# Attention of a fused encoder trunk: samples taken two by two, a head pair's values beside the scores of pair p+2, and scores and values of the same tile shape in one visit of TensorE

## The chip, the cores and the metric

The kernel runs on one core of one Trainium2 chip. The metric is device time in microseconds (us) of one execution. Engines are called as the profile calls them: PE (TensorE), DVE (VectorE), ACT (ScalarE), POOL (GpSimd) and SP (SyncE, which issues DMAs).

## The reference

Two layers of an encoder trunk, on 512 tokens of one prompt and 8 x 16 tokens of eight running samples (640 tokens of width 1024) with shared weights. Cut to what matters:

```python
# per layer: x += SwiGLU_1(norm(x))/2 ; mixer ; x += SwiGLU_2(norm(x))/2
z = h @ w_in          # conv B | C | V, q | k | v, two gates
def _band_attention(q, k, v, q_pos, k_pos, rel_bias):
    s = jnp.einsum('bqhd,bkhd->bhqk', q, k) * (HEAD_DIM ** -0.5)
    s = s + rel_bias[:, idx][None]
    s = jnp.where(valid[None, None], s, NEG_INF)     # chunk-causal band
    p = jax.nn.softmax(s, axis=-1)
    return jnp.einsum('bhqk,bkhd->bqhd', p, v)
# prompt: 512 queries on their own 512 keys; 8 heads of 64
# sample b: 16 queries on 256 cached keys and its 16 new ones
m = sigmoid(g_c) * (y_c @ w_conv_out) + sigmoid(g_a) * (y_a @ w_attn_out)
x += m @ w_o
```

## The kernel before

All is fp32. A large product is made of three: each operand is split into a high part (hi) and a rest (lo), and PE adds hi*hi, lo*hi and hi*lo (`block`, L395). Weights come in slabs: SP loads a `raw` block (L245, three buffers), ACT casts it to `whi` (L305), DVE subtracts to get `wlo` (L310, in one or two pieces), and some slabs are sums of blocks (L249, tiles `raw` and `s`). PE takes a whole layer's products as such slabs of 128x128 weights over two halves of 320 tokens; `seven` makes a 2x2 block product of seven half-size ones, with DVE adding the partial results (L249, for instance `g <- mb_g`) and ACT copying them (L716, L724, L728).

Attention is woven into this. Inside the mixer PE's order is the order in which the code is written. The other engines' order is made by a scheduler from priorities: `soon()` raises one by 300, a weight slab has 150. `attention()` holds a generator, `stream`, with all products that don't hang on attention (q and k of head pairs 1 to 3, the convolutions, the gates), cut in 140 steps of six matmuls of 128x320. `fill(n)` lets PE run n steps. Between fills PE visits attention. The eight heads go in four pairs, the two heads of a pair in two halves of the array:

- `scores(p)`: q x k for the row blocks 0 to 3 of 128 queries, 128 to 512 keys wide, on tiles of 64 rows by 128 columns (L1669). The results (`pss`) are read by DVE, which adds the bias and takes the maximum (L1675); then the negative maximum (L1826), ACT's exponentials (L1828), DVE's reciprocal (L1831), and ACT's scaling (L1686). Odd pairs hold them in tiles `s`, even pairs in `yc`.
- `values(p)`: transposes of the weights (L1699) in two stops of 14 and 6, copied out to `pt` by DVE (first head) and ACT (second, L1702). Then values x weights, here called PV, on tiles of 128 rows by 64 columns (L1713, result `py`, copied by ACT at L1715).
- `sscores(b)`: a sample's scores, tiles of 128x32 (L1757, `spss`); its caches `kc`, `vc` and new values `vn` are loaded on SP (L1746, L1749, L1752), in the queue that also loads the weights.
- `svalues(b)`: three transposes (L1779, L1781, `sptp`), copied out by ACT and DVE (L1783, L1784); then the values of the 16 new keys on tiles of 16x32 and of the cached keys on tiles of 128x32 (both L1791, `spy`), ACT's scaling, and a transpose (L1797, `ptx`, one bank for four samples).

All attention results share four PSUM banks (`att`), in turn; the stream's `ma`, `mb`, `mc` and the scores of row block 1 have the four others (`pr`). The profile lists each of these fp32 attention matmuls as two records, and joins neighbours of one shape on the timeline ("x16"). Before, the prompt's order per pair is scores(p+1), four steps, transposes, two steps, transposes, two steps, PV, six steps. A sample's is four steps, transposes, three steps, then in one visit the scores of sample b+2 and the values of sample b, two steps, last transpose.

Of the kernel before, what the change touches and what calls it, by code (L numbers as in the profile page):

```python
# [12 lines left out]
AF = mybir.ActivationFunctionType  # L13
# [3 lines left out]
P = 128  # L17
D = 1024
L = 2
SEQ = 512  # L20
NB = 8
TS = 16
T = SEQ + NB * TS
HT = T // 2
PAST = 256
H = 8
HD = 64
# [153 lines left out]
def trunk(ctx: ExitStack, tc: tile.TileContext, xin, wst, small, pbias, samplebias, kcache, vcache,  # L181
          yout, ko, vo, co):
    nc = tc.nc
    PE, DVE, ACT, POOL, SP = nc.tensor, nc.vector, nc.scalar, nc.gpsimd, nc.sync
# [8 lines left out]
    ps = ExitStack()  # L193
# [15 lines left out]
    def att(name):  # L209
        return banks["att"].tile([P, 512], F32, tag="att", name=name)  # L210
# [15 lines left out]
    for kind, inside in kinds():  # L226
        n = len(fourth)
# [137 lines left out]
    def soon():  # L365
        return tc.high_priority(offset=300)
# [34 lines left out]
    ident = cp.tile([P, P], F32, name="ident")  # L401
# [12 lines left out]
    for k in range(KT):  # L414
# [4 lines left out]
        if k % 2 == 0:  # L419
            c = slice(k * P, (k + 2) * P)  # L420
# [693 lines left out]
    def mixer(l, after):  # L1114
        with tc.tile_pool(name=f"yp{l}", bufs=1, reuse_waits="tile") as yp, \
# [19 lines left out]
            with tc.tile_pool(name=f"mp{l}", bufs=2, reuse_waits="tile") as mp:  # L1135
# [63 lines left out]
                with tc.manual_schedule(engines={mybir.EngineType.PE}):  # L1199
                    attention(l, h, st, stats, ops, mp, yas, ycp, both, others())  # L1200
# [368 lines left out]
    def attention(l, h, norms, stats, ops, mp, yas, ycp, both, others):  # L1569
# [3 lines left out]
        npair = H // 2  # L1573
        nt = T // P
        NQ = SEQ // P
        KS = PAST + TS
# [29 lines left out]
        def fill(n):  # L1606
            for _ in range(n):
                next(stream, None)
# [5 lines left out]
        for c in range(KT // 2):  # L1614
            wh, wl = chunk()
            for kk in range(2):
# [29 lines left out]
        def scores(p):  # L1646

            heads = [2 * p + e for e in range(2)]
            bias, ss, st = [], [], []
            for hh in heads:  # L1650
                n = f"{l}_{hh}"
                bias.append(mp.tile([P, SEQ], F32, name=f"bias{n}", tag="bias"))
                POOL.dma_start(bias[-1], pbias[l, hh])
                POOL.memset(bias[-1][0:CHUNK, SEQ - CHUNK :], NEG)

                ss.append(mp.tile([P, offs[-1] + SEQ], F32, name=f"s{n}", tag="s") if p % 2
                          else ycp[hh % 2].rearrange("p a t -> p (a t)"))
                st.append(mp.tile([P, 4, NQ], F32, name=f"st{n}", tag="st", bufs=4))

            for rows in ((0, 2), (3,), (1,)):  # L1660
                pss = [(pr if rows == (1,) else att)(f"pss{l}_{hh}_{rows[0]}") for hh in heads]
                spans, o = [], 0
                for i in rows:
                    spans.append((i, slice(o, o + (i + 1) * P)))
                    o = spans[-1][1].stop
                for i, c in spans:
                    for e in range(2):
                        r = slice(e * HD, (e + 1) * HD)
                        PE.matmul(pss[e][:, c], qa[p][r, i * P : (i + 1) * P], ka[p][r, : (i + 1) * P],  # L1669
                                  start=True, stop=True)  # L1670
                for i, c in spans:
                    for e in range(2):
                        w = (i + 1) * P
                        with soon():
                            DVE.tensor_tensor_reduce(  # L1675
                                out=ss[e][:, offs[i] : offs[i] + w], in0=pss[e][:, c],
                                in1=bias[e][:, SEQ - w :], scale=1.0, scalar=NEG, op0=ALU.add,
                                op1=ALU.max, accum_out=st[e][:, 0, i : i + 1])
            for e, hh in enumerate(heads):
                weigh(hh, ss[e], st[e])  # L1680

        def weigh(hh, s, st):
            parts = [(offs[i], (i + 1) * P) for i in range(NQ)]
            softmax(s, st, parts)
            for i, (o, w) in enumerate(parts):
                ACT.activation(s[:, o : o + w], s[:, o : o + w], AF.Copy, scale=st[:, 3, i : i + 1])  # L1686
            weights[hh] = s

        def values(p):

            pt = [mp.tile([P, offs[-1] + SEQ], F32, name=f"pt{l}_{2 * p + e}", tag="pt") for e in range(2)]
            at = [sum(P * (NQ - i) for i in range(j)) for j in range(NQ)]

            def turn(j, e):
                w = (NQ - j) * P
                s = weights[2 * p + e]
                ptp = att(f"ptp{l}_{2 * p + e}_{j}")[:, :w]
                for i in range(j, NQ):
                    PE.transpose(ptp[:, (i - j) * P : (i - j + 1) * P],  # L1699
                                 s[:, offs[i] + j * P : offs[i] + (j + 1) * P], ident)  # L1700
                with soon():
                    (ACT.copy if e else DVE.tensor_copy)(pt[e][:, at[j] : at[j] + w], ptp)  # L1702

            for j in range(NQ):
                for e in range(2):
                    turn(j, e)
                if j % 2:
                    yield
            py = att(f"py{l}_{p}")
            for j in range(NQ):  # L1710
                for e in range(2):
                    hh = 2 * p + e
                    PE.matmul(py[e * HD : (e + 1) * HD, j * P :], vs[j][:, hh * HD : (hh + 1) * HD],  # L1713
                              pt[e][:, at[j] : at[j] + (NQ - j) * P], start=j == 0, stop=j == NQ - 1)
            ACT.copy(yas[:, p, 0:SEQ], py)  # L1715
# [24 lines left out]
        def sscores(b):  # L1740
# [28 lines left out]
                    ACT.activation(early, st[:, 3, 0:1], AF.Sigmoid)  # L1769
            held[b] = box, st, vraw, vn  # L1770

        def svalues(b):
            n = f"{l}_{b}"
            box, st, vraw, vn = held[b]
            s = box[:, :KS]
            pt = box[:, KS : KS + 2 * P].rearrange("p (a b) -> p a b", a=2)
            pn, yx = (box[:n, KS + o * P : KS + (o + 1) * P] for n, o in ((TS, 2), (P, 3)))
            ptp = att(f"sptp{n}")
            for j in range(2):  # L1779
                PE.transpose(ptp[:, j * P : (j + 1) * P], s[:, j * P : (j + 1) * P], ident)  # L1780
            PE.transpose(ptp[:TS, 2 * P : 3 * P], s[:, PAST:], ident)  # L1781
            with soon():
                ACT.copy(pt, ptp[:, : 2 * P].rearrange("p (a b) -> p a b", a=2))  # L1783
                DVE.tensor_copy(pn, ptp[:TS, 2 * P : 3 * P])  # L1784
            yield

            pys = att(f"spy{n}")[:, :P]
            for j, (w, v) in enumerate(((pn, vn), (pt[:, 0], vraw[:, 0]), (pt[:, 1], vraw[:, 1]))):
                for p in range(npair):
                    r = slice(32 * p, 32 * p + 32)  # L1790
                    PE.matmul(pys[r], w[:, r], v[:, p * P : (p + 1) * P], start=j == 0, stop=j == 2)  # L1791
# [6 lines left out]
            if b % G == G - 1:  # L1798
                c0 = SEQ + (b + 1 - G) * TS
                for e in range(2):  # L1800
                    r = slice(e * HD, (e + 1) * HD)
                    with soon():
                        (ACT.copy if e else DVE.tensor_copy)(
                            yas[r, :, c0 : c0 + G * TS].rearrange("p a (b t) -> p a b t", b=G),
                            ptx[0][r].rearrange("p (b a e t) -> p a b e t", b=G, a=npair, e=2)[:, :, :, e, :])

        sscores(0)
        sscores(1)
        for b in range(NB):
            vals = svalues(b)  # L1810
            fill(4)
            next(vals)
            fill(3)
            if b + 2 < NB:
                sscores(b + 2)
            next(vals)
            fill(2)
            next(vals, None)
        fill(KT * KT)

    def softmax(s, st, parts):
# [304 lines left out]
```

## Time and profile before

| | us |
|---|---|
| median of 3 runs (2495.63 to 2496.84) | 2496.47 |
| the profiled execution, whole | 2496.66 |
| its span, first to last instruction | 2494.7 |
| PE busy | 2478.1 |
| DVE busy | 2119.2 |
| ACT busy | 1450.0 |
| POOL busy | 370.7 |

The profiled execution is 1.96 us longer than its span, and 0.19 us above the median. The granted TensorE clock is 0.998 of full speed. Busy time of PE is modelled from pipelined matmuls, so a busy PE need not run at its peak; the distance from the start of one matmul to the start of the next shows that. The woven part of layer 0 lies at about 475 to 650 us of the span, that of layer 1 some 1233 us later.

### The profile page before, as it was taken

What the parts mean: (1) busy time and instruction counts of PE and PEld (TensorE: products, weight loads), DVE (VectorE), ACT (ScalarE), POOL (GpSimd) and SP (SyncE); (2) the same over time, 40 slices, a digit from 0 to 9 for tenths busy, and PEclk for the clock granted to TensorE, in tenths of its full rate; (3) what the DMA queues carried; (4) which work ended last, traced back from release to release, by engine and by line L of the source; (5) the groups of instructions that cost most, each with busy time, mean ns of one, the idle gap of its engine ahead of it and who ended that gap; (6) DMA issues with size and microseconds to landing.
All of it is one profiled execution on the core that took longest, in us unless ns stands there. A gap on an engine that the chain in (4) does not pass through costs nothing.

```text
span 2494.7 us, 43515 instructions
## 1 busy us (share of the span) xinstructions
PE 2478.1 (99%) x17048; PEld 2419.0 (97%) x17048; DVE 2119.2 (85%) x3322; ACT 1450.0 (58%) x2343; POOL 370.7 (15%) x445
## 2 busy tenths in 40 slices
PE   9999999999999999999999999999999999999998
PEld 8999999888999999999999999998899999999998
DVE  7888888878888899888798889888788888989887
ACT  7455556674666555555565555556646665555554
POOL 0011211211111011111001111221111110111111
PEclk9999999999999999999999999999999999999999
DMA  4245665335345344655435555643344553455554
GB/s 146 82 107 124 138 135 130 106 115 167 99 119 145 101 116 118 138 135 135 117 90 126 129 134 123 138 119 115 125 153 104 126 141 95 119 133 122 129 135 110
DMA packets 133261, 308.10 MB, mean 124 GB/s; under 512 B 12768, under 2 KB 76128, under 8 KB 133056
## 3 DMA queue, kind: packets, MB, share of 16 engines
q1 hardware_dynamic: 68976, 219.18, 27.3%
q0 software_dynamic: 63360, 85.50, 20.6%
q8 instruction: 133, 2.18, 0.4%
q10 hardware_dynamic: 720, 0.65, 0.1%
q14 instruction: 72, 0.59, 0.1%
HBM read 221.13 MB, written 7.94 MB: 92 GB/s over the span
## 4 chain that ended last, share of the span: by engine, by line
PE 94%; DVE 3%; ACT 2%; DMA 1%; issue 0%; SPq 0%; DVEq 0%; ACTq 0%
PE pab L395 12%; PE paa L395 11%; PE pcb L395 6%; PE pca L395 6%; PE daa L962 5%; PE dab L962 5%; PE po L372 4%; PE qa L395 4%; PE pbb L395 3%; PE pba L395 3%; PE dca L962 3%; PE dcb L962 3%; PE pda L372 2%; PE pv L1622 2%; PE ma_cv L395 2%; PE qc L395 2%
## 5 line engine op out<-in xcount | busy, mean ns | idle before, releaser
L310 DVE TENSOR_TENSOR wlo<-raw,whi 128x512 fp32r<-128x512 f32 (+1 forms) x583 | 598.6, 1030 | 236.1 <-ACT whi L305 230.6
L305 ACT CAST whi<-raw 128x512 fp32r<-128x512 f32 (+1 forms) x583 | 519.9, 897 | 348.0 <-PE pbb L395 44.6
L305 ACT CAST whi<-s 128x1024 fp32r<-128x1024 f32 (+1 forms) x164 | 153.6, 937 | 248.1 <-issue 107.8
L395 PE MATMUL pab<-xhib,whi 128*128 128x320 f32 x704 | 218.3, 310 | 0.4 <-DVE gb L249 0.4
L395 PE MATMUL pab<-xhib,wlo 128*128 128x320 f32 x704 | 217.4, 309 | 0.0
L395 PE MATMUL pab<-xlob,whi 128*128 128x320 f32 x704 | 217.4, 309 | 0.0
L395 PE MATMUL paa<-xhia,whi 128*128 128x320 f32 x640 | 198.0, 309 | 0.2 <-DVE ga L249 0.2
L395 PE MATMUL paa<-xloa,whi 128*128 128x320 f32 x640 | 197.6, 309 | 0.0
L395 PE MATMUL paa<-xhia,wlo 128*128 128x320 f32 x640 | 197.6, 309 | 0.0
L310 DVE TENSOR_TENSOR wlo<-s,whi 128x1024 fp32r<-128x1024 f32 (+1 forms) x164 | 176.6, 1077 | 10.4 <-ACT whi L305 10.4
L395 PEld LDWEIGHTS pab<-xhib,whi 128*128 128x128 f32 x704 | 132.2, 188 | 1.1 <-DVE gb L249 0.9
L395 PEld LDWEIGHTS pab<-xlob,whi 128*128 128x128 f32 x704 | 132.2, 188 | 0.2
L395 PEld LDWEIGHTS pab<-xhib,wlo 128*128 128x128 f32 x704 | 132.2, 188 | 0.0
L395 PEld LDWEIGHTS paa<-xhia,whi 128*128 128x128 f32 x640 | 120.2, 188 | 0.5 <-DVE ga L249 0.5
L395 PEld LDWEIGHTS paa<-xloa,whi 128*128 128x128 f32 x640 | 120.2, 188 | 0.1
L395 PEld LDWEIGHTS paa<-xhia,wlo 128*128 128x128 f32 x640 | 120.2, 188 | 0.0
L249 DVE TENSOR_TENSOR raw<-raw,raw 128x512 f32<-128x512 f32 x164 | 112.2, 684 | 1.8 <-DMA raw<-in_wst 0.2
L249 DVE TENSOR_TENSOR raw<-s,raw 128x512 f32<-128x512 f32 x164 | 112.3, 685 | 0.0
L395 PE MATMUL pcb<-xhib,whi 128*128 128x320 f32 x352 | 108.7, 309 | 0.0
L395 PE MATMUL pcb<-xlob,whi 128*128 128x320 f32 x352 | 108.7, 309 | 0.0
L395 PE MATMUL pcb<-xhib,wlo 128*128 128x320 f32 x352 | 108.7, 309 | 0.0
L986 POOL DMA_DIRECT2D x<-c_b x52 | 62.6, 1203 | 309.5 <-ACT c_b L979 134.5
(816 smaller groups left out, 8170.8 us busy)
## 6 DMA issues: line engine op xcount, KB each, us to landing
raw<-in_wst SPq DMA_DIRECT2D x375, 512.0 KB, 3.7
x<-c_b POOLq DMA_DIRECT2D x52, 320.0 KB, 5.1
x<-c_a POOLq DMA_DIRECT2D x50, 320.0 KB, 5.0
kc<-in_kcache SPq DMA_DIRECT2D x32, 256.0 KB, 4.1
vc<-in_vcache SPq DMA_DIRECT2D x16, 512.0 KB, 4.5
ub<-cbb POOLq DMA_DIRECT2D x42, 160.0 KB, 5.9
ua<-cba POOLq DMA_DIRECT2D x38, 160.0 KB, 5.4
x<-u_a POOLq DMA_DIRECT2D x18, 320.0 KB, 5.1
```

The costliest lines, as they stand in the source:

```text
L249: DVE.tensor_tensor(out=out, in0=a, in1=b, op=ALU.add)
L305: ACT.copy(hi[:, d], src[:, c])
L310: DVE.tensor_tensor(out=lo, in0=src, in1=hi.bitcast(F32), op=ALU.subtract)
L372: PE.matmul(ps[a] if isinstance(ps, list) else ps[:, a, :HT], w, x[:, a * HT : (a + 1) * HT], start=first and j == 0, stop=last and j == 2)
L395: PE.matmul(ps, a, b, start=start and kp == 0 and j == 0, stop=stop and kp == NP - 1 and j == 2, skip_group_check=True)
L962: PE.matmul(ps[u], w, y, start=start and i == 0 and j == 0, stop=i == 1 and j == 2, skip_group_check=True)
L986: POOL.dma_start(rows(r, cols), z, accum_op=ALU.add)
L1622: PE.matmul(pv[t], xx[:, t * P : (t + 1) * P], w[:, kk * AW : (kk + 1) * AW], start=c == 0 and kk == 0 and j == 0, stop=c == KT // 2 - 1 a ...
```

## The change

Five edits in `attention()`:

1. `scores` takes the row blocks in the order 0, 2, 1, 3 (before 0, 2, 3, 1).
2. The copy of `py` gets the raised priority.
3. PV of pair p is put off: it stands right ahead of scores(p+2), with no step between; PV of the last pair stands right ahead of the first two samples' scores. The transposes keep their places relative to the scores.
4. Samples go in pairs. One visit holds the scores of samples b+2 and b+3, the values of the cached keys of b and b+1, and then those of their new keys.
5. `ptx` holds two samples instead of four, so it is copied out four times per layer instead of twice (by DVE and ACT each time).

The number of steps, of products and of DMAs is the same. Cut to its core:

```diff
@@ scores(p) @@
-            for rows in ((0, 2), (3,), (1,)):
+            for rows in ((0, 2), (1,), (3,)):
...
@@ the end of values(p) @@
-            ACT.copy(yas[:, p, 0:SEQ], py)
+            with soon():
+                ACT.copy(yas[:, p, 0:SEQ], py)
             yield
@@ the schedule of the prompt @@
+        vals = None
         fill(2)
         scores(0)
         fill(14)
         for p in range(npair):
+            if vals:
+                next(vals)
             if p + 1 < npair:
                 scores(p + 1)
-                fill(4)
+            fill(4 if p + 1 < npair else 2)
             vals = values(p)
             next(vals)
             fill(2)
             next(vals)
-            fill(2)
-            next(vals)
-            fill(6)
+            fill(8)
+        next(vals)
...
-        G = 4
+        G = 2
@@ svalues: of one sample before, of two now @@
-        def svalues(b):
...
-            ptp = att(f"sptp{n}")
-            for j in range(2):
-                PE.transpose(ptp[:, j * P : (j + 1) * P], s[:, j * P : (j + 1) * P], ident)
-            PE.transpose(ptp[:TS, 2 * P : 3 * P], s[:, PAST:], ident)
-            with soon():
-                ACT.copy(pt, ptp[:, : 2 * P].rearrange("p (a b) -> p a b", a=2))
-                DVE.tensor_copy(pn, ptp[:TS, 2 * P : 3 * P])
+        def svalues(bs):
...
+            for b, box, pt, pn in zip(bs, boxes, pts, pns):
+                s = box[:, :KS]
+                ptp = att(f"sptp{l}_{b}")
...
+                with soon():
+                    ACT.copy(pt, ptp[:, : 2 * P].rearrange("p (a b) -> p a b", a=2))
+                    DVE.tensor_copy(pn, ptp[:TS, 2 * P : 3 * P])
             yield
-            pys = att(f"spy{n}")[:, :P]
-            for j, (w, v) in enumerate(((pn, vn), (pt[:, 0], vraw[:, 0]), (pt[:, 1], vraw[:, 1]))):
-                for p in range(npair):
-                    r = slice(32 * p, 32 * p + 32)
-                    PE.matmul(pys[r], w[:, r], v[:, p * P : (p + 1) * P], start=j == 0, stop=j == 2)
-            with soon():
-                ACT.activation(yx, pys, AF.Copy, scale=st[:, 3, 0:1])
+            pys = [att(f"spy{l}_{b}")[:, :P] for b in bs]
+            for js in ((0, 1), (2,)):
+                for b, ps, pt, pn in zip(bs, pys, pts, pns):
+                    vraw, vn = held[b][2:]
+                    for j in js:
+                        w, v = (pn, vn) if j == 2 else (pt[:, j], vraw[:, j])
+                        for p in range(npair):
+                            r = slice(32 * p, 32 * p + 32)
+                            PE.matmul(ps[r], w[:, r], v[:, p * P : (p + 1) * P], start=j == 0, stop=j == 2)
+            for b, ps, yx in zip(bs, pys, yxs):
+                with soon():
+                    ACT.activation(yx, ps, AF.Copy, scale=held[b][1][:, 3, 0:1])
             yield
-            if b % G == 0:
-                ptx[0] = att(f"ptx{n}")
-            PE.transpose(ptx[0][:, (b % G) * P : (b % G + 1) * P], yx, ident)
...
+            for b, yx in zip(bs, yxs):
+                if b % G == 0:
+                    ptx[0] = att(f"ptx{l}_{b}")[:, : G * P]
+                PE.transpose(ptx[0][:, (b % G) * P : (b % G + 1) * P], yx, ident)
...
@@ the schedule of the samples @@
         sscores(0)
         sscores(1)
-        for b in range(NB):
-            vals = svalues(b)
+        fill(7)
+        for b in range(0, NB, 2):
+            vals = svalues((b, b + 1))
+            next(vals)
+            fill(5)
+            for c in range(b + 2, min(b + 4, NB)):
+                sscores(c)
+            next(vals)
             fill(4)
-            next(vals)
-            fill(3)
-            if b + 2 < NB:
-                sscores(b + 2)
-            next(vals)
-            fill(2)
             next(vals, None)
+            fill(9 if b + 2 < NB else 0)
         fill(KT * KT)
```

The lines of the changed kernel lie 1 lower from the copy of `py` on, 3 from the samples' loads on, up to 7 and 9 in `svalues`, and 10 from the softmax on: L1760 is `spss`, L1798 is `spy`, L1836 is the negative maximum.

First, PE in layer 0 where the scores of sample 2 are taken (`ma0_b0`, `mc0_b0` are the stream's products, `spss0_2` the scores of sample 2, `spy0_0` the values of sample 0, `vc` its cached and `vn` its new ones). Before:

```order
3282 L395 MATMUL ma0_b0_6175<-thi0_1_4685,wlo147_6142 128x320
3283 L1757 MATMUL spss0_2_6229<-kc0_2_0_6219,bd0_4707 32x272 x2
3284 L1757 MATMUL spss0_2_6229<-kc0_2_1_6221,bd0_4707 32x272 x2
3285 L1791 MATMUL spy0_0_6240<-vn0_0_6095,ss0_0_6104 32x128 x4
3286 L1791 MATMUL spy0_0_6240<-vc0_0_6093,ss0_0_6104 32x128 x8
3287 L395 MATMUL ma0_b0_6175<-thi0_2_4687,whi147_6141 128x320
```

After:

```order
3326 L395 MATMUL mc0_b0_6220<-hhim0_7_4652,wlo148_6172 128x320
3327 L1760 MATMUL spss0_2_6288<-kc0_2_0_6278,bd0_4707 32x272 x2
3328 L1760 MATMUL spss0_2_6288<-kc0_2_1_6280,bd0_4707 32x272 x2
3329 L1760 MATMUL spss0_3_6309<-kc0_3_0_6299,bd0_4707 32x272 x2
3330 L1760 MATMUL spss0_3_6309<-kc0_3_1_6301,bd0_4707 32x272 x2
3331 L1798 MATMUL spy0_0_6320<-vc0_0_6121,ss0_0_6132 32x128 x8
3332 L1798 MATMUL spy0_1_6321<-vc0_1_6142,ss0_1_6153 32x128 x8
3333 L1798 MATMUL spy0_0_6320<-vn0_0_6123,ss0_0_6132 32x128 x4
3334 L1798 MATMUL spy0_1_6321<-vn0_1_6144,ss0_1_6153 32x128 x4
3335 L395 MATMUL ma0_b0_6175<-thi0_0_4683,whi149_6203 128x320
```

Two samples' scores and values stand in one run without a stream matmul between, and the new keys' matmuls have moved behind the cached keys'.

Second, DVE in layer 0 where it works on the scores of pair 1 (`pss0_2`, `pss0_3` are the scores of its two heads, the number behind a row block; `st` holds maxima and sums; ACT's exponentials wait for the row of L1826, now L1836). Before:

```order
627 L1675 ISA s0_2_5270,st0_2_5271<-pss0_2_1_5293,bias0_2_5267 128x256
628 L1675 ISA st0_2_5271 128x1
629 L1675 ISA s0_3_5275,st0_3_5276<-pss0_3_1_5294,bias0_3_5272 128x256
630 L1675 ISA st0_3_5276 128x1
631 L1826 TENSOR_SCALAR st0_2_5271<-st0_2_5271 128x4
632 L310 TENSOR_TENSOR wlo132_5251<-raw74_5184,whi132_5250 128x1024
633 L1826 TENSOR_SCALAR st0_3_5276<-st0_3_5276 128x4
```

After:

```order
626 L1675 ISA s0_2_5270,st0_2_5271<-pss0_2_3_5293,bias0_2_5267 128x512
627 L1675 ISA st0_2_5271 128x1
628 L310 TENSOR_TENSOR wlo131_5227<-raw75_5220,whi131_5226 128x512
629 L1836 TENSOR_SCALAR st0_2_5271<-st0_2_5271 128x4
630 L1675 ISA s0_3_5275,st0_3_5276<-pss0_3_3_5294,bias0_3_5272 128x512
631 L1675 ISA st0_3_5276 128x1
632 L310 TENSOR_TENSOR wlo132_5251<-raw74_5184,whi132_5250 128x1024
633 L1836 TENSOR_SCALAR st0_3_5276<-st0_3_5276 128x4
```

The last row block is now the widest, the first head's negative maximum stands ahead of the second head's last block, and a piece of the weight slab `wlo131` stands ahead of that.

Third, DVE in layer 0 at the first gate's products (`wlo163` is the second weight slab of that block, `g0_0` the gate, `mb0_g0` its second product on PE). Before:

```order
867 L310 TENSOR_TENSOR wlo163_6932<-s6_90_6927,whi163_6931 128x512
868 L1189 TENSOR_TENSOR b0_2_6779<-b0_2_6779,rrm0_4681 128x640
869 L1149 SCALAR_TENSOR_TENSOR b0_3_6780<-ma0_b2_6786,rrm0_4681 128x320
870 L1190 TENSOR_TENSOR yc0_4682<-yc0_4682,b0_2_6779 128x640
871 L1193 TENSOR_TENSOR yc0_4682<-yc0_4682,b0_3_6780 128x640
872 L1784 COPY ss0_6_6744<-sptp0_6_6949 16x128
873 L310 TENSOR_TENSOR wlo163_6932<-raw91_6925,whi163_6931 128x512
874 L249 TENSOR_TENSOR raw90_6889<-s6_90_6927,raw90_6889 128x512
875 L249 TENSOR_TENSOR g0_0_6958<-mb0_g0_6979,capsm0_4680 128x320
876 L310 TENSOR_TENSOR wlo164_6962<-raw90_6889,whi164_6961 128x1024
```

After:

```order
872 L249 TENSOR_TENSOR raw91_6930<-raw91_6930 128x512
873 L249 TENSOR_TENSOR g0_0_6957<-mb0_g0_6978,capsm0_4680 128x320
874 L310 TENSOR_TENSOR wlo163_6937<-s6_90_6932,whi163_6936 128x512
875 L310 TENSOR_TENSOR wlo163_6937<-raw91_6930,whi163_6936 128x512
876 L249 TENSOR_TENSOR raw90_6890<-s6_90_6932,raw90_6890 128x512
```

The sum `g0_0<-mb0_g0`, which waits for PE to end `mb0_g0`, stood behind both pieces of `wlo163` and now stands ahead of both. Layer 1 has the same two orders at this place.

More of the change, by code (lines that the diff above doesn't have):

```diff
@@ L1770, in sscores @@
             held[b] = box, st, vraw, vn
-        def svalues(b):
[L1773 to L1777, printed above, removed]
-            ptp = att(f"sptp{n}")
-            for j in range(2):
-                PE.transpose(ptp[:, j * P : (j + 1) * P], s[:, j * P : (j + 1) * P], ident)
-            PE.transpose(ptp[:TS, 2 * P : 3 * P], s[:, PAST:], ident)
-            with soon():
-                ACT.copy(pt, ptp[:, : 2 * P].rearrange("p (a b) -> p a b", a=2))
-                DVE.tensor_copy(pn, ptp[:TS, 2 * P : 3 * P])
-            yield
-            pys = att(f"spy{n}")[:, :P]
-            for j, (w, v) in enumerate(((pn, vn), (pt[:, 0], vraw[:, 0]), (pt[:, 1], vraw[:, 1]))):
-                for p in range(npair):
-                    r = slice(32 * p, 32 * p + 32)
-                    PE.matmul(pys[r], w[:, r], v[:, p * P : (p + 1) * P], start=j == 0, stop=j == 2)
-            with soon():
-                ACT.activation(yx, pys, AF.Copy, scale=st[:, 3, 0:1])
-            yield
-            if b % G == 0:
-                ptx[0] = att(f"ptx{n}")
-            PE.transpose(ptx[0][:, (b % G) * P : (b % G + 1) * P], yx, ident)
[L1798 to L1805, printed above, removed]
```

14 lines of the change are left out of this document (added).

## The prediction, made before the changed kernel was run

> **What bounds the kernel now.** I read the page first: the span, the busy shares and the chain that ended last.
>
> ```profile
> span 2494.7 us, 43515 instructions
> PE 2478.1 (99%) x17048; PEld 2419.0 (97%) x17048; DVE 2119.2 (85%) x3322; ACT 1450.0 (58%) x2343; POOL 370.7 (15%) x445
> ...
> PE 94%; DVE 3%; ACT 2%; DMA 1%; issue 0%; SPq 0%; DVEq 0%; ACTq 0%
> ```
>
> PE is all but never idle, and 94% of the chain is PE's. Then I read what PE waits for.
>
> ```profile
> PE poa L372 <- ACT whi L618: 5.6, 1, 5.6
> ...
> PE ptp L1699 <- ACT pt L1702: 0.8, 4, 0.3
> ```
>
> The columns are us in total, times, longest. The largest wait lies outside attention; in attention only the transposes wait, four times. So time is gained or lost where PE's own run of matmuls gets shorter or where a new wait holds it. A busy PE says little, so next I read PE's timeline by starts: how far apart are two starts, and how does that change around a visit to attention? This is the PV visit of pair 0.
>
> ```profile
> 499.44 0.31 PE L395 MATMUL ma_qk<-thi,wlo 128*128 128x320 f32 x1
> ...
> 500.32 0.31 PE L395 MATMUL ma_qk<-thi,wlo 128*128 128x320 f32 x1
> 500.56 2.37 PE L1713 MATMUL py<-pt,v 128*64 128x512 f32 x16
> 502.87 0.42 PE L395 MATMUL mc_qk<-hhim,whi 128*128 128x320 f32 x1
> 503.12 0.31 PE L395 MATMUL mc_qk<-hlom,whi 128*128 128x320 f32 x1
> ```
>
> Six starts from 499.44 to 500.32 make 0.147 us for a stream matmul. Into the visit the distance is 0.24, and behind it the first stream matmul takes 0.25 to the next start: 0.09 and 0.10 us too much. So a visit has a price of its own beside its work. The samples' visits show the price inside.
>
> ```profile
> 561.83 0.31 PE L395 MATMUL mc_cv<-hhim,wlo 128*128 128x320 f32 x1
> 562.07 1.12 PE L1757 MATMUL spss<-kc,bd 128*32 128x272 f32 x16
> 563.12 0.41 PE L395 MATMUL ma_cv<-thi,whi 128*128 128x320 f32 x1
> ```
> ```profile
> 569.58 0.31 PE L395 MATMUL ma_b<-thi,wlo 128*128 128x320 f32 x1
> 569.81 0.67 PE L1757 MATMUL spss<-kc,bd 128*32 128x272 f32 x8
> 570.41 0.42 PE L1791 MATMUL spy<-vn,ss 16*32 16x128 f32 x8
> 570.76 0.64 PE L1791 MATMUL spy<-vc,ss 128*32 128x128 f32 x16
> 571.34 0.42 PE L395 MATMUL ma_b<-thi,whi 128*128 128x320 f32 x1
> 571.59 0.31 PE L395 MATMUL ma_b<-tlo,whi 128*128 128x320 f32 x1
> ```
>
> Sixteen records of `spss` take 1.05 to the next start, eight take 0.60: eight more cost 0.45, and 0.15 is left over for going to the next shape. Eight records of `spy` on 16x32 take 0.35, sixteen on 128x32 take 0.58: 0.23 for eight, 0.12 left over. I take 0.13 for leaving a shape; then eight records of `spss` are 0.46 and eight of `spy` 0.22.
>
> **The change part by part**, for one layer; both layers have the same code.
>
> *Samples, three full visits.* One visit of before is 571.59 - 569.58 less two stream matmuls, 1.72; two are 3.43. The paired visit has one way in (0.08), 16 `spss` (0.92), 32 `spy` of cached keys in the same tile shape (0.90), 16 of new keys (0.45), two leavings (0.26) and one way out (0.10): 2.71. It saves 0.72, three times 2.17. That the pair's 48 records of one shape carry no price between `spss` and `spy` is an assumption; if they paid 0.13, 0.4 would be lost.
>
> *Samples, the last pair, without new scores.* One is 0.08 + 0.22 + 0.13 + 0.45 + 0.13 + 0.10 = 1.11, two 2.22; the pair is 0.08 + 0.90 + 0.13 + 0.45 + 0.13 + 0.10 = 1.79: 0.43.
>
> *Prompt.* Three visits go: PV of pairs 0 and 1 join scores, PV of pair 3 the first samples' scores. A join saves a way in and a way out, 0.09 + 0.10, if going directly from one shape to the next costs the 0.13 of a leaving. No row shows 128x64 followed by 64x128. The ends are 0.32 (free) and 0 (as dear as in, leaving and out). I take 0.19, as the small shapes beside each other are the nearest rows: 0.57. The Trainium skill, TensorEngine Tiling (Array Packing), Key Properties, says that a change of tiling mode drains the TensorE and a change of tile alone does not. By that rule alone, with one price for every change, in and out are two drains of 0.16 and a join saves 0.48 in place of 0.57; the trace agrees that each change costs, but puts the price mostly at the 128x128 side.
>
> Transposes are moved, not shortened, and I count nothing for them. So the switches give 2.17 + 0.43 + 0.57 = 3.17.
>
> *Stalls that may go.* The second stop of transposes and one visit of scores:
>
> ```profile
> 498.04 0.83 PE L1699 MATMUL ptp<-ident,yc 128*128 128x128 f32 x6
> 498.63 0.39 PE L395 MATMUL ma_qk<-thi,whi 128*128 128x320 f32 x1
> ```
> ```profile
> 517.63 0.38 PE L1699 MATMUL ptp<-ident,s 128*128 128x128 f32 x2
> 518.17 0.70 PE L1699 MATMUL ptp<-ident,s 128*128 128x128 f32 x4 [0.17 <-ACT pt L1702]
> 518.63 0.40 PE L395 MATMUL ma_qk<-thi,whi 128*128 128x320 f32 x1
> ```
> ```profile
> 537.76 0.38 PE L1699 MATMUL ptp<-ident,yc 128*128 128x128 f32 x2
> ...
> 538.87 0.39 PE L395 MATMUL ma_cv<-thi,whi 128*128 128x320 f32 x1
> ```
> ```profile
> 528.12 0.31 PE L395 MATMUL ma_cv<-hhim,wlo 128*128 128x320 f32 x1
> 528.49 2.43 PE L1669 MATMUL pss<-k,q 64*128 64x128 f32 x16
> ```
>
> Pair 0 needs 0.59 for its six, pair 1 1.00, pair 2 1.11: stalls of 0.41 and 0.52, waits for ACT's copies. The scores of pair 3 begin 0.37 after the matmul ahead instead of 0.24: 0.13. Why are the copies late?
>
> ```profile
> 508.22 1.81 DVE L310 TENSOR_TENSOR wlo<-raw,whi 128x512 fp32r<-128x512 f32 x2
> 509.95 0.28 DVE L1675 CUSTOM_DVE_ANT_0 yc<-pss,bias 128x128 f32<-128x128 f32 x1
> ```
> ```profile
> 513.43 0.40 ACT L1828 ACTIVATE yc<-yc,st 128x128 f32<-128x128 f32 x1 [4.55 <-DVE st L1826]
> ```
>
> DVE is at `wlo` until 509.95 while PE began these scores about 508.3, and ACT, idle for 4.55, begins its exponentials only at 513.43; the copies queue behind them. With PV ahead of the scores PE gives DVE 2.3 us for that `wlo`, and the first head's maximum no longer stands behind the second head's last block. Against it, ACT now scales four blocks ahead of the copies rather than two. The ends are 0 and 0.41 + 0.52 + 0.13 = 1.06; I take 0.70, as DVE's gain of up to 1.6 is the larger. If the cover is not there the stalls stay.
>
> *A stall that comes.* At the first gate `g <- mb_g` now stands ahead of `wlo163` on DVE. PE and DVE there, before, and the duration of such a piece:
>
> ```profile
> 632.24 0.31 PE L395 MATMUL ma_g<-thi,whi 128*128 128x320 f32 x1
> ...
> 632.53 0.31 PE L395 MATMUL ma_g<-thi,wlo 128*128 128x320 f32 x1
> ```
> ```profile
> 632.51 0.49 DVE L249 TENSOR_TENSOR g<-mb_g,capsm 128x320 f32<-128x320 f32 x1 [1.60 <-PE mb_g L395]
> 632.91 1.22 DVE L310 TENSOR_TENSOR wlo<-raw,whi 128x1024 fp32r<-128x1024 f32 x1
> ```
> ```profile
> L310 DVE TENSOR_TENSOR wlo<-s,whi 128x512 fp32r<-128x512 f32 x44 | 30.3, 689 | 7.2 <-ACT whi L305 7.2
> ```
>
> The sum starts when `mb_g` has ended (632.51), the next on DVE at 632.91, and a piece of `wlo` takes 0.69: ready at 633.60. PE wants it in its third matmul, 632.53. That is 1.1 us of standing still, on the path; behind it on DVE wait the second piece and the next slab. Ends 0.7 (a piece starting early and pipelined) and 1.8 (both pieces).
>
> *The rest costs nothing that I can see.* Two more small copies of `ptx` on DVE and ACT per layer lie beside PE's stream; uncovered, four of the size of the sum above would be 2 us per layer. POOL's copies of the samples' keys and its loads of the bias move with the scores; POOL is busy for 15% of the span, and nothing on PE's list waits for it. SP's loads keep their number; their place is a rival below.
>
> The sum per layer is -3.17 - 0.70 + 1.10 = -2.77, twice -5.5. The profiled execution took 2496.66, so 2491.1; the median lies 0.19 lower: **2490.9 us**.
>
> **The rivals.**
>
> *Copies out of PSUM become the limit.* `att` has four banks. In scores(2) and scores(3) the second head's last block takes the bank of `py`, which PE has just filled, and waits for ACT's copy.
>
> ```profile
> 556.73 0.59 ACT L1715 COPY ya<-py 128x512 f32<-128x512 f32 x1 [1.91 <-PE py L1713]
> ```
>
> For it: the copy takes 0.59, and on ACT a cast of a slab stands ahead of it. Against: about half of the scores' 2.3 us, 1.2 to 1.4, lies between PV and that block, so ACT may be 0.6 late unpunished. If it is 1 us later, four visits lose 4 us; with the stalls kept instead, 1.4 is lost. Both leave a gain of about 2 to 4: 2493.5. The Trainium skill, TensorEngine Tiling (Array Packing), PSUM Bottleneck, speaks against the change in this sense: tiling speeds up TensorE and not the evacuation of PSUM, and the copies may become the limit.
>
> *The switches give more and the stall stays small.* Direct changes are free (0.39 more per layer), the stalls go whole (0.36) and the gate waits for 0.7: 3.17 + 0.39 + 1.06 - 0.7 = 3.92 per layer, 2488.6; without the gate's wait 2487.2.
>
> *Weights come late: slower.* On SP the weights' `raw` loads stand behind the samples' loads, which wait for buffers that a visit frees.
>
> ```profile
> SPq L1746 <- PE spss L1757: 51.3, 8, 7.6
> ```
>
> Two samples' loads now wait for one later visit. If the `raw` behind them are late, PE stands at the next slab. For it: waits of up to 7.6 us on that queue. Against: PE's list shows no wait for a weight there, so 7.6 are covered. To end 5 us slower, six paired visits (three per layer) would have to lose (5.5 + 5) / 6 = 1.75 us each, so the queue would have to hold the `raw` that much longer than its cover; 1.9 each gives 2502.3.
>
> **How the numbers follow.** A measurement of this kernel can tell about 0.2%, 5.0 us, from no change. The forecast gets 0.58, the copies' rival 0.22, the larger gain 0.13, late weights 0.07. The forecast's own range is 2489.4 (all three stalls gone, the gate's wait 0.7) to 2492.3 (none gone); the bound of 2491.5 lies in it, so I give 0.45 of its 0.58 to faster, and 0.13 to same. Faster 0.45 + 0.13 = 0.58; same 0.13 + 0.22 = 0.35; slower 0.07. The range 2487.2 to 2494.6 goes from the larger gain to the copies' rival with one more us lost.
>
> **What would show it right or wrong.** Right: on PE's timeline a paired sample visit of about 2.7 us without stream matmuls, and about 1.8 for the last; PV followed by scores at once with less than 0.35 between the last PV start and the first score beyond its own work; the six transposes of pairs 1 and 2 near 0.6; and `ma_g` waiting for `wlo` L310 in PE's waits, about 1.1, twice. Wrong: a start-to-start price of 0.3 or more at each shape change inside a visit; `pss` waiting for `py`'s copy; `whi` or `raw` in PE's list of waits at the samples; or a granted clock below 0.998.

## The result and the profile after

The changed kernel is slower by a little: 2500.93 us median (2499.94 to 2502.43, 17 runs) against 2496.54 (2495.6 to 2497.3, 17 runs), a ratio of 1.0018 with a 95% interval of 1.0011 to 1.0024. Forecast were 2490.9 and a range of 2487.2 to 2494.6. The profiled execution took 2501.16 us, its span is 2499.4.

The page of the changed kernel, the lines shown of before:

```profile
span 2499.4 us, 43503 instructions
PE 2474.7 (99%) x17048; PEld 2422.0 (97%) x17048; DVE 2119.0 (85%) x3326; ACT 1453.0 (58%) x2347; POOL 366.3 (15%) x445
...
PE 90%; DVE 5%; ACT 3%; issue 1%; DMA 1%; SPq 0%; DVEq 0%; ACTq 0%
```

PE's busy time fell by 3.4 us while the span grew by 4.7. PE has less to do and stands still more; in the chain that ended last, PE's share went from 94 to 90%, and that of DVE and ACT rose by 3 points together. What PE waits for (us in total, times, longest):

```profile
PE poa L372 <- ACT whi L618: 5.6, 1, 5.6
PE ma_qk L395 <- DVE k L249: 4.1, 4, 1.0
PE ma_cv L395 <- DVE yc L249: 2.1, 2, 1.1
...
PE ma_g L395 <- DVE wlo L310: 0.8, 2, 0.4
...
PE ma_g L395 <- ACT whi L305: 0.6, 2, 0.3
```

The wait of the transposes for `pt` has gone from this list; four lines are new. The wait at `ma_g` for `wlo` was forecast, that for `whi` and those at `ma_qk` and `ma_cv` were not. The last two are six waits, three per layer, 1.0 to 1.1 each. The first of them on PE, DVE and ACT:

```profile
498.24 0.93 PE L1699 MATMUL ptp<-ident,yc 128*128 128x128 f32 x6
498.93 0.39 PE L395 MATMUL ma_qk<-thi,whi 128*128 128x320 f32 x1
...
500.77 0.41 PE L395 MATMUL mc_qk<-hhim,whi 128*128 128x320 f32 x1
...
502.49 0.31 PE L395 MATMUL mc_qk<-hhim,wlo 128*128 128x320 f32 x1
503.81 0.42 PE L395 MATMUL ma_qk<-thi,whi 128*128 128x320 f32 x1 [1.01 <-DVE k L249]
504.06 0.31 PE L395 MATMUL ma_qk<-tlo,whi 128*128 128x320 f32 x1
```
```profile
498.66 0.69 DVE L1702 COPY pt<-ptp 128x256 f32<-128x256 f32 x2 [0.86 <-PE ptp L1699]
502.13 1.23 DVE L310 TENSOR_TENSOR wlo<-raw,whi 128x1024 fp32r<-128x1024 f32 x1 [2.78 <-ACT whi L305]
503.27 0.48 DVE L249 TENSOR_TENSOR k<-ma_qk,c 128x320 f32<-128x320 f32 x1
```
```profile
500.61 0.54 ACT L1702 COPY pt<-ptp 128x256 f32<-128x256 f32 x2
501.03 1.06 ACT L305 CAST whi<-raw 128x1024 fp32r<-128x1024 f32 x1
```

Read them from the bottom. ACT, with exponentials, scalings and the copies of the transposes ahead, casts a weight slab only at 501.03. DVE has nothing to do for 2.78 us, because the `wlo` of that slab is next in its order. Behind it stands the sum `k<-ma_qk`, whose operand PE had finished by about 500.9. PE wants to write the next product into the same bank at 502.64, may at 503.81 (1.17 too late), and loses another 0.10 on the step after that. In the kernel before the same sum stood behind the same `wlo`, but PV lay between the transposes and this point (500.56 to 502.87 in the rows of the prediction), and PE came to the bank later than the sum ended:

```profile
499.60 1.04 ACT L305 CAST whi<-raw 128x1024 fp32r<-128x1024 f32 x1
```
```profile
502.54 0.48 DVE L249 TENSOR_TENSOR k<-ma_qk,c 128x320 f32<-128x320 f32 x1
```
```profile
504.73 0.31 PE L395 MATMUL ma_qk<-thi,whi 128*128 128x320 f32 x1
```

All three rows are of before. The sum ended at about 502.95, PE came at 504.73: 1.8 to spare. Afterwards 1.2 are lacking, and two things make the difference: PE comes 2.1 sooner (502.64 instead of 504.73), and the sum, behind a cast that starts 1.4 later (501.03 instead of 499.60), starts 0.7 later (503.27 instead of 502.54, where a sum of raw blocks stood between).

The visits themselves came out as forecast:

```profile
507.29 0.31 PE L395 MATMUL ma_qk<-hhim,wlo 128*128 128x320 f32 x1
507.52 2.38 PE L1713 MATMUL py<-pt,v 128*64 128x512 f32 x16
509.83 2.43 PE L1669 MATMUL pss<-k,q 64*128 64x128 f32 x16
512.19 0.41 PE L395 MATMUL mb_qk<-hhim,whi 128*128 128x320 f32 x1
512.44 0.31 PE L395 MATMUL mb_qk<-hlom,whi 128*128 128x320 f32 x1
```
```profile
579.37 0.31 PE L395 MATMUL mc_b<-hhim,wlo 128*128 128x320 f32 x1
579.61 1.12 PE L1760 MATMUL spss<-kc,bd 128*32 128x272 f32 x16
580.55 1.06 PE L1798 MATMUL spy<-vc,ss 128*32 128x128 f32 x32
581.53 0.64 PE L1798 MATMUL spy<-vn,ss 16*32 16x128 f32 x16
582.10 0.42 PE L395 MATMUL ma_b<-thi,whi 128*128 128x320 f32 x1
582.36 0.31 PE L395 MATMUL ma_b<-tlo,whi 128*128 128x320 f32 x1
```

PV and scores together: 512.44 - 507.29 less two stream matmuls, 4.86 against 2.50 + 2.55 apart. The paired visit: 2.70 against 3.43. At the gate PE stands as follows:

```profile
632.11 0.31 PE L395 MATMUL mb_g<-hhim,wlo 128*128 128x320 f32 x1
632.72 0.41 PE L395 MATMUL ma_g<-thi,whi 128*128 128x320 f32 x1 [0.30 <-ACT whi L305]
...
633.67 0.42 PE L395 MATMUL ma_g<-thi,wlo 128*128 128x320 f32 x1 [0.39 <-DVE wlo L310]
```

An account of layer 0, from PE's starts between the same two stream matmuls (470 and 650 of before; all visits, then all distances of the stream over 0.147):

| us | before | after |
|---|---|---|
| visits to attention, with their stalls | 47.43 | 43.83 |
| gaps in the stream over 0.15 | 0 | 4.91 |
| rest of the stream | 132.57 | 133.23 |
| sum | 180.01 | 181.97 |

The gaps are 1.17, 1.20, 1.22 (bank `ma`), 0.30, and 0.47 and 0.55 at the gate; the rest grew by 0.66, of which 0.6 is the 0.10 behind each of the six. So 3.6 are won and 5.6 lost. Layer 1 has the same six gaps to within 0.01, and 181.85 against 179.92. Together 3.9 of the span's 4.7. The remainder of 0.8 lies outside them, in stretches of products that differ by 0.2 to 0.3 either way and behind the last matmul; nothing shows that it belongs to the change.

### The profile page after: what moved, and what is told of

Read it like the earlier page. It is cut to its first block, busy times and chain, and to the rows that moved or that the text cites. A ratio compares the mean times of both kernels' runs of the same rounds, so it can differ in the third digit from the quotient of the medians.

```text
span 2499.4 us, 43503 instructions
## 1 busy us (share of the span) xinstructions
PE 2474.7 (99%) x17048; PEld 2422.0 (97%) x17048; DVE 2119.0 (85%) x3326; ACT 1453.0 (58%) x2347; POOL 366.3 (15%) x445
## 4 chain that ended last, share of the span: by engine, by line
PE 90%; DVE 5%; ACT 3%; issue 1%; DMA 1%; SPq 0%; DVEq 0%; ACTq 0%
PE pab L395 12%; PE paa L395 11%; PE pcb L395 6%; PE pca L395 6%; PE daa L962 5%; PE dab L962 5%; PE qa L395 4%; PE po L372 4%; PE pbb L395 3%; PE pba L395 3%; PE dcb L962 3%; PE dca L962 3%; PE pda L372 2%; PE pv L1622 2%; PE qc L395 2%; PE poa L372 2%
```

## The experiments

Two theories stood against each other. A: at its old place PV covered the time in which ACT and DVE free the banks `mc` and `ma` behind the transposes; moved, it covers nothing. B: the new row order changes what ACT does first, and its late cast is what PE waits for. C blames the samples' part. The sum of layer 0, between the same matmuls, is called "layer 0" below; "transposes" are the visits of `ptp` in that account, stalls included (9.74 before, 9.58 after). Every ratio is to the kernel before on the same chip.

**PV back at its old place, all else changed**

```diff
             next(vals)
-            fill(8)
-        next(vals)
+            fill(2)
+            next(vals)
+            fill(6)
```

(and no `next(vals)` ahead of the scores).

> The changed kernel, with PV of each pair put back to its old place: two steps behind the second stop of transposes, six steps ahead of the next scores. Row order, samples two by two and all else as in the changed kernel; the places on DVE and ACT of the casts, the wlo pieces and the sums around the transposes are those of the changed kernel. Theory A (lost cover): PV stood between the transposes and the next product into bank ma, and while PE ran it (2.3 us and the ways in and out) ACT made the late cast, DVE its wlo and then the sum that frees the bank. Then the three gaps of 1.2 us per layer go, with 0.1 us each for starting again, and the three joins of PV are given back (0.2 each): per layer 3.9 gained, 0.6 lost, so about 2500.9 - 6.6 = 2494.3. Theory B (late cast): the new row order put ACT's cast behind the copies, and PE waits for it wherever PV stands: the gaps stay near 1.2 and the time is about 2502.

Measured: 2496.07, ratio 0.9997 (0.9988 to 1.0006); layer 0 179.85. None of the three gaps of 1.2 is left, and ACT's cast is no earlier in ACT's order than in the changed kernel. ACT's cast, DVE's sum and PE's arrival at the bank:

```profile
500.42 1.06 ACT L305 CAST whi<-raw 128x1024 fp32r<-128x1024 f32 x1
```
```profile
502.66 0.48 DVE L249 TENSOR_TENSOR k<-ma_qk,c 128x320 f32<-128x320 f32 x1
```
```profile
504.41 0.31 PE L395 MATMUL ma_qk<-thi,whi 128*128 128x320 f32 x1
```

That is A. The three small gaps (0.29, and 0.47 and 0.54 at the gate) stay. But 1.8 us of the expected gain are missing. The transposes and scores stall more than in any other kernel:

```profile
517.57 0.60 PE L1699 MATMUL ptp<-ident,s 128*128 128x128 f32 x4
518.45 0.70 PE L1699 MATMUL ptp<-ident,s 128*128 128x128 f32 x2 [0.29 <-ACT pt L1702]
518.91 0.39 PE L395 MATMUL ma_qk<-thi,whi 128*128 128x320 f32 x1
```

1.34 for six transposes, against 1.00 before. With PV in its old place the two visits' stalls and those of the scores sum to 0.96 per layer more than before. This is the price of the new row order: the transposes take 10.42 here against 9.74 with the old rows and PV at the same place, and with PV put off 9.58 against the 8.99 of the next run. My reading is that four scalings ahead of ACT's copies, instead of two, make it, and that in the changed kernel the gaps at `ma` give ACT time; no run separates these.

**Old row order, all else changed**

```diff
-            for rows in ((0, 2), (1,), (3,)):
+            for rows in ((0, 2), (3,), (1,)):
```

> The changed kernel with the row blocks in the old order 0, 2, 3, 1; nothing else. On ACT the cast of the slab in question stands ahead of the second pair of copies again (as before the change), on DVE one sum of raw blocks now stands between wlo and the sum that frees ma. Theory A: PE still comes 2.5 us sooner to ma than before the change; cast 499.8 to 500.9, wlo to 502.1, the sum of raw to 502.7, the sum to 503.1: the gaps shrink to about 0.6 and do not go. Per layer 3 x 0.6 gained, with the transposes' stalls 0.1 to 0.2 worse: about 2497.6. Theory B: no gaps are left, per layer 3.9 gained: about 2493.4.

Measured: 2497.6, ratio 1.0004 (0.9995 to 1.0013); layer 0 180.31. The time is that of A, but by luck, and the place is not. PE waits one bank earlier:

```profile
PE mc_qk L395 <- ACT c L728: 2.7, 4, 0.7
PE mc_cv L395 <- ACT c L728: 1.5, 2, 0.7
```

Gaps of 0.80, 0.89 and 0.89 per layer: with the cast ahead of it, ACT's copy of the old content of `mc` is now what is late. Putting the cast earlier on ACT does not remove the wait, it hands it to the copy behind the cast. The gaps shrink by 1.0 per layer in place of the expected 1.8, and the transposes take 0.6 less in place of 0.1 to 0.2 more. B, which wants no gaps, falls; what is short is ACT's time between the transposes and these banks. But the new order is not free: with the old one the changed kernel is 3.3 us faster (2497.6 against 2500.93).

**The samples' part alone**

The prompt as before, the samples' functions and schedule as changed:

```diff
-        G = 4
+        G = 2
...
-        def svalues(b):
+        def svalues(bs):
...
-        for b in range(NB):
-            vals = svalues(b)
+        fill(7)
+        for b in range(0, NB, 2):
+            vals = svalues((b, b + 1))
...
```

> The kernel before with the samples' part of the change alone (two by two, one bank of ptx for two samples); prompt as before. Theory A: none of the three gaps of 1.2, since the prompt keeps PV's place; the paired visits save 2.23 + 0.46 per layer, and at the gate the first piece of wlo stands ahead of the sum again, so that at most 0.3 to 0.8 of the smaller gaps is left: -5.4 + 0.6 to 1.6, 2491.7 to 2492.7. Rival C (the samples' part is what costs, by weights that come late): no faster than 2496.5.

Measured: 2490.67, ratio 0.9976 (0.9967 to 0.9985); layer 0 177.19. There is no gap at all, and the visits are 2.70 shorter per layer (47.43 to 44.73): all that the pairs save arrives, and C falls. It is a us faster than expected, as the smaller gaps are gone too.

**Transposes two steps later**

```diff
-            fill(4 if p + 1 < npair else 2)
+            fill(6 if p + 1 < npair else 4)
...
-            fill(8)
+            fill(6)
```

> The changed kernel with both stops of transposes two steps later and PV two steps closer (six steps behind the transposes instead of eight). Steps and visits are the same in number. On ACT the cast then stands ahead of the first copies and on DVE wlo stands between the copies, the sum that frees ma behind the last copy. Theory A: the latency is moved away from the reuse of ma; cast and wlo are early, and the sum waits for two copies of 0.7 us together behind the second stop: gaps of 0 to 0.4, about 2493 to 2496. Theory B gives the same or less; what tells is whether PE then waits at the transposes (ptp for pt) instead.

Measured: 2500.46, ratio 1.0015 (1.0006 to 1.0024); layer 0 181.68. A miss of 4 us and more. The gaps at `ma` shrank nearly as far as expected, to below 0.15, 0.48 and 0.47, but other waits came or grew:

```profile
PE qa L395 <- ACT ya L1812: 2.7, 2, 1.4
PE ma_g L395 <- DVE wlo L310: 1.1, 2, 0.8
...
PE ptp L1699 <- ACT pt L1702: 1.0, 2, 0.5
```

The transposes wait up to 0.5 for copies that on ACT now stand behind the cast, and at the end of the woven part PE's product `qa` waits 1.4 for ACT's copy of `ptx`. In the changed kernel ACT makes that copy as late, 1.4 behind the start of the transpose (646.15 and 644.72; here 644.22 and 642.80), but there PE starts `qa` at 644.85 without it. So what differs is not ACT but that `qa` has to wait for that copy here, perhaps because it got the same bank; no run shows why.

**PV two steps later in the kernel before**

```diff
             next(vals)
-            fill(2)
+            fill(4)
             next(vals)
-            fill(6)
+            fill(4)
```

> The kernel before with one edit: PV of each pair two steps later (four steps behind the second stop of transposes and four ahead of the next scores, instead of two and six). No join, old row order, samples one by one; ACT and DVE have the order of the kernel before around it. Theory A (PV covers the copies): PE comes without PV to the next product into bank mc, whose old content ACT copies (L728) only behind the late cast and a copy of the transposes; in the kernel before that copy ended at 501.2, and PE would want the bank at about 500.5: gaps of 0.7 to 0.9, three per layer, 0.1 each for starting again: 5 to 6 us slower, about 2502. Theory B (the new row order's late cast): nothing has changed that matters, about 2496.7.

Measured: 2500.99, ratio 1.0017 (1.0008 to 1.0026); layer 0 182.01. Two steps' difference in PV's place, with no join, the old rows and the old samples, make the kernel as slow as the change does. PE and ACT:

```profile
500.02 0.31 PE L395 MATMUL ma_qk<-thi,wlo 128*128 128x320 f32 x1
500.97 0.41 PE L395 MATMUL mc_qk<-hhim,whi 128*128 128x320 f32 x1 [0.65 <-ACT c L728]
...
502.92 1.40 PE L1713 MATMUL py<-pt,v 128*64 128x512 f32 x6
```
```profile
499.29 1.04 ACT L305 CAST whi<-raw 128x1024 fp32r<-128x1024 f32 x1
500.23 0.37 ACT L1702 COPY pt<-ptp 128x256 f32<-128x256 f32 x1
500.49 0.43 ACT L728 COPY c<-mc_qk 128x320 f32<-128x320 f32 x1
```

ACT does the same in the same order as before the change. PV at 502.92 now lies behind `mc`, no longer ahead of it; the gaps are 0.81, 0.89, 0.89. This is A by itself. It is a us less than expected, because the visits' stalls shrink by 0.91 per layer (46.52 against 47.43 us; the transposes alone 8.99 against 9.74).

**The prompt's part alone**

```diff
-            for rows in ((0, 2), (3,), (1,)):
+            for rows in ((0, 2), (1,), (3,)):
...
+            if vals:
+                next(vals)
             if p + 1 < npair:
                 scores(p + 1)
...
+            fill(8)
+        next(vals)
```

> The kernel before with the prompt's part of the change alone: new row order, priority of the copy of py, PV put off to stand beside scores, PV of the last pair beside the first sample's scores; samples one by one. Theory A: three gaps of 1.2 and three restarts of 0.1 per layer, less 0.6 for the joins and 0.2 to 0.3 for the smaller stalls; the samples save nothing: (3.9 - 0.9) x 2 = 6.0 slower, 2502.5 to 2503, and with the gate's waits (1.2 per layer) if they come, 2505. Additivity with the samples alone (6.3 faster) would then give about the changed kernel's 2501 only with the gate's and the samples' small waits (1.5 per layer) on top. Rival C (the samples' part costs): faster than 2496.

Measured: 2503.85, ratio 1.0027 (1.0017 to 1.0038); layer 0 183.80. PE's waits have the changed kernel's lines at `ma_qk` and `ma_cv`, none at `ma_g`, and one of the last sample's, which the expectation had not named:

```profile
PE ma_qk L395 <- DVE k L249: 4.1, 4, 1.1
PE ma_cv L395 <- DVE yc L249: 2.1, 2, 1.0
PE ptx L1800 <- ACT ss L1796: 1.6, 2, 0.8
```

By their medians the samples alone are 6.3 faster and the prompt alone 7.1 slower; added up that is 0.8 slower, and both together give 4.4. The 3.6 between are an interaction. By the accounts of layer 0 it is 1.96 - (3.79 - 2.82) = 1.0 per layer, so 2 of the 3.6; the rest is not placed. The last run below looks at the gate's part in it.

**Transposes ten steps behind the scores**

```diff
-            fill(4 if p + 1 < npair else 2)
+            fill(10 if p + 1 < npair else 6)
...
-            fill(8)
+            fill(2)
```

With the new row order, and again with the old one. At this place the convolution overwrites `yc` before the weights of pair 2 are read from it, so pair 2 is computed from other numbers; instructions and sizes are the same.

> The changed kernel with the transposes put six steps later relative to the scores (10 steps from scores to the first stop instead of 4, the last pair 6), and PV two steps behind the second stop as in the kernel before. So PV keeps its cover of the reuse of mc and stands directly ahead of scores(p+2) all the same; row order, samples in twos as changed. On ACT the cast and on DVE wlo and the sum that frees ma stand ahead of the copies of the transposes; at the gate one piece of wlo stands ahead of the sum. Theory A: none of the three gaps; the joins (0.6 per layer) and the samples (2.7) are kept, the transposes' stalls of before (0.9) go as the copies have no exponentials ahead: per layer -3.3 to -4.2, 2488 to 2490. Theory B: the cast is early here too, so no gaps; the same. A wait of pt for PV or of ya's copy at the end would show as less gain.

> The same with the old row order 0, 2, 3, 1. Theory A: the order of rows matters only by what queues ahead of the copies on ACT; with transposes ten steps behind the scores nothing of it is late: equal to the run with the new row order within 1 us, 2488 to 2490. Theory B: the old order puts the cast earlier, so faster than the run with the new order by over 1 us.

Measured: 2493.32, ratio 0.9986 (0.9977 to 0.9995), and 2492.8, ratio 0.9985 (0.9976 to 0.9994); layer 0 178.32 and 178.10. The stalls at the second stop of the transposes of pairs 1 and 2 are gone (a new one of 0.15 and 0.34 stands at the first stop of pair 2) and the joins kept, but the stream waits for another of ACT's copies:

```profile
497.13 0.41 PE L395 MATMUL ma_qk<-thi,whi 128*128 128x320 f32 x1 [0.41 <-ACT capsm L724]
```

Gaps of 0.57, 0.91 and 0.91 with the new rows, 0.81, 0.59 and 0.58 with the old. My reading that without transposes nothing on ACT is late was wrong: the exponentials of the new scores are enough. The order of rows makes 0.5 us, as A says; the time itself A missed by 3 us.

**The samples' part and one join**

```diff
             next(vals)
-            fill(2)
-            next(vals)
-            fill(6)
+            if p + 1 < npair:
+                fill(2)
+                next(vals)
+                fill(6)
+            else:
+                fill(8)
+                next(vals)
```

> The kernel before with the samples two by two, as in the run of the samples alone, and of the prompt's part only one join: PV of the last pair eight steps behind its transposes, directly ahead of the first samples' scores. Behind the last pair no softmax follows on ACT, so theory A has no late cast there and no gap: 0.2 more per layer than the samples alone, 2490.3. If a gap of 0.8 to 1.3 came there too, 2492 to 2493.3, and the joining itself would be what costs.

Measured: 2490.12, ratio 0.9976 (0.9966 to 0.9985); layer 0 177.00, 0.19 less than the samples alone, as expected, and no gap. Joining by itself is not what costs. This version beats both kernels, by 6.6 us against before; against the samples alone the runs' ranges overlap.

**Two steps fewer ahead of the last pair's transposes, all else changed**

```diff
-            fill(4 if p + 1 < npair else 2)
+            fill(4 if p + 1 < npair else 0)
```

> The changed kernel with two steps fewer ahead of the last pair's transposes (68 steps in the prompt's part as before the change, 70 in the samples'). On DVE one piece of wlo stands ahead of the gate's sum again. Theory A for the remainder: the gate's waits come from the two steps by which all samples stand later in the stream, and go (0.47 + 0.55 and two restarts, 1.2 per layer, and the smaller one of 0.3): 2500.9 - 3.0 = 2497.9, with the three gaps of 1.2 still there. If the pairs of samples themselves make the gate late, no change: 2500.9.

Measured: 2497.16, ratio 1.0001 (0.9992 to 1.001); layer 0 180.27. The gaps at the gate and the one of 0.30 are gone, the three of 1.2 are not (1.18, 1.21, 1.22). So the gate's waits come from two steps of fill in the prompt's part together with samples in pairs: the pairs without the steps (the samples' part alone) and the steps without the pairs (the prompt's part alone) do not have them. Where the samples stand in the stream decides whether the scheduler puts the gate's sum ahead of `wlo`. The two steps are worth 3.8 (2500.93 - 2497.16), 1.70 per layer by the account of layer 0. That this is near the interaction of 3.6 proves little, as the prompt's part alone has a wait at its last sample that no other run has.

## Why the prediction was wrong, point by point

- **What bounds the kernel**: held. PE's run of matmuls and what holds it made every difference.
- **Samples**: right. 2.23 and 0.46 per layer against 2.17 and 0.43. That 48 records of one tile shape carry no price between two products held: `spss` to `spy` takes 580.55 - 579.61 = 0.94 for sixteen.
- **Prompt, joins**: right. 0.19 each (PV and scores 5.05 to 4.86, PV and `spss` 3.75 to 3.55), 0.58 against 0.57. The Trainium skill, TensorEngine Tiling (Array Packing), Key Properties, says that a change of tiling mode drains the TensorE. The trace agrees that each change has a price; with one price for all a join would have saved 0.16, and it saves 0.19.
- **Stalls that go**: the term was mis-sized. 0.30 per layer instead of 0.70: pair 0 0.10 worse, pair 1 from 1.00 to 0.92, pair 2 from 1.11 to 0.92, the scores' 0.13 gone. And not for the reason given: the new order, from which the prediction hoped for a gain, makes them 0.96 worse by the run with PV put back. What gains is PV's move, and PV two steps later with no join gains as much (8.99 against 9.74), where PE stands at `mc` instead.
- **The stall at the gate**: right in place and size, 0.47 + 0.55 = 1.02 for 1.1, but part of it is a wait for `whi`, which the prediction had named only as a sign of being wrong, and each restart costs 0.10 on top. It needs the two steps of fill and the samples in pairs together.
- **"The rest costs nothing that I can see"**: this step failed. Costing PV's move, I counted what it saves where it goes and never asked what it hid where it stood. I named a cover for the small copies of `ptx`, and none for the block that moved. PV's 2.4 us were the cover of ACT's copy of `mc` and of DVE's sum on `ma`. The price is three gaps of 1.2 and three restarts, 3.9 per layer, more than all that the switches saved (3.27). The new row order has a part in it, which the prediction had weighed for the stalls alone: with the old order the same move costs three gaps of 0.8 to 0.9. Put back one by one, PV's place is worth 4.9 us of the whole, the row order 3.3 and the two steps 3.8; they do not add up, as the first two act on the same three places.
- **The rivals**: of the copies out of PSUM I looked only at `py`, and no wait of `pss` for it shows; the raised priority of that copy was not tested by itself. In kind the rival was near: what runs short is the time in which ACT and DVE free banks, but the stream's, not attention's. The Trainium skill, TensorEngine Tiling (Array Packing), PSUM Bottleneck, says that tiling speeds up TensorE and not the evacuation of PSUM. Here it was not a matter of speed: a block of PE's work was moved, and the gaps of 1.17 to 1.22 are at a bank of the stream's 128x128 products. Late weights on SP: no `raw` is waited for; the weight that was late was late on ACT (the cast at 501.03). The rival on the slower side had a queue of the wrong engine: not SP's, but ACT's.

The sum with the measured sizes: -3.27 - 0.30 + 1.22 (gate with restarts) + 3.9 + 0.4 (the gap of 0.30 with its restart) = 1.95 per layer, and layer 0 shows 1.96.

## What to carry to other kernels

A block of PE work that is moved takes its cover along: before moving it, list every bank and buffer that the next few steps behind its old place reuse, and read from the trace how long before PE's arrival each is freed. A margin of 1.8 us with a block of 2.4 us in front of it is a deficit once the block goes. And where the engine that empties PSUM is short of time after a burst, reordering its work can pass the wait on to the next reader in its queue: three gaps of 1.2 became three of 0.8 to 0.9 at another bank.

## What the runs showed of the hardware that I had not expected

Behind each of the six gaps of a layer the next distance between two stream matmuls was 0.25 instead of 0.147, a tenth of a microsecond for starting again, as much as behind a change of tile shape. A direct change from 128x64 to 64x128 took no more than a leaving to the full array: PV's sixteen records took 2.31 us to the next start in both cases (507.52 to 509.83, and 500.56 to 502.87 before).
